# Operand sums built in the second feed-forward's first tiles, one ordinary tile ahead of its second down stage, transposes in pieces, and DRAM sums issued at other steps

## The chip, the cores and the metric

The kernel runs on one core of one Trainium2 chip. The metric is the time of one launch on the device in microseconds (us), as the median of several runs. The core's engines work through queues of their own: PE (TensorE: matrix products into PSUM, and transposes), DVE (VectorE), ACT (ScalarE), POOL (GpSimd) and SP (SyncE, which only starts DMAs). An instruction waits at the head of its queue until its inputs are there and its output buffer is free, and everything behind it on that engine waits with it.

## The reference

One decoder layer on 512 tokens of width 1024, all in float32. The change lies in the last line but one, and in what runs under the line with the mixers:

```python
h = h + FFN_HALF * _swiglu(_rmsnorm(h, norm_ffn1[i]), ffn1_gate[i], ffn1_up[i], ffn1_down[i])
# two attention mixers (native sparse and sliding window), gated and merged:
h = h + merged @ w_out[i]
h = h + FFN_HALF * _swiglu(_rmsnorm(h, norm_ffn2[i]), ffn2_gate[i], ffn2_up[i], ffn2_down[i])
return _rmsnorm(h, norm_final)

def _swiglu(x, w_gate, w_up, w_down):
    return (jax.nn.silu(x @ w_gate) * (x @ w_up)) @ w_down
```

The inner width D_FF is 2816, which is 22 tiles of 128 columns.

## The kernel before, in words

**Products in three passes.** A float32 operand is held as a high part, rounded to the matrix unit's format, and a low part, the rest. A product is three matmuls: high by high, low by high, high by low (`mm3`, L711; `mm` at L386). Splitting an operand costs ACT a copy (the high part) and DVE a subtraction (the low part). A block of weights (128 x 1024 values, 512 KB) is read from DRAM by SP into `raw` and split into `whi` (ACT, L150) and `wlo` (DVE, L154). `W.next()` hands PE the next block and, as it is called, puts the split of the block two places ahead into the queues of ACT and DVE. There are four places for split blocks and four raw buffers.

**Activations.** `uh` and `ul` are the high and low part of h times the norm's gain, 8 blocks of 128 x 512, transposed (features on partitions, tokens along the row). The norm's factor per token is applied later. `norm_in` (L654 to L655) makes them block by block, `square` adds up the squares (ACT, then POOL at L666 into `sqacc`), and `norm_col` and `norm_rows` turn the sum into the factor, with a few small matmuls (printed as `tp`), a chain of tiny DVE steps and one POOL power.

**The output projection.** Eight blocks d = 0 to 7, each 24 matmuls; then DVE adds the result to h (L1763), `norm_in` follows, and for d = 4 to 7 `sums_of_tokens(d - 4)` (L1747 to L1758): from h it forms four combinations of token halves and feature blocks, and splits them into `four_hi` and `four_lo`. They are operands of the fast matrix products of the next stage.

**The second feed-forward** goes over three groups of tiles (0 to 7, 8 to 15, 16 to 21). An *ordinary* tile is 24 matmuls by its gate block, 24 by its up block, and `gated` (L1791 on: DVE takes z from the gate's PSUM bank, ACT silu, DVE t from the up's bank, DVE the product, then a split into rows of `G` or into operands). Tiles 8 to 11, 12 to 15 and 16 to 19 are done four at a time by `four` (L1826 to L1932): seven products of half-size matrices in place of eight, in the order 1, 5, 6, 3, 7, 2, 4, each in two blocks of 12 matmuls (L1857), with tokens on the partitions. Some weight operands of these products are sums of weight blocks that were added up in DRAM beforehand, by DMAs that POOL starts. Results then have to be turned back by transposes (`tp<-ident`, L1889): `pair_rows` turns two tiles' worth, ACT copies them out, and `operands_of` (L1905 to L1916: four DVE combinations, two ACT copies, two DVE subtractions) makes seven operands of the down product from them. Work that is to be put between later matmuls waits in the list `turns`; `turn_back()` takes one entry. Values that `later` holds are put out after the next `W.next()`: the gating of the tokens (L1843).

**Down products.** After the first and the second group, `down` multiplies a group of eight tiles in 14 steps of 12 matmuls with seven-product operands, `left_hi` (rows 0 to 13 of `G`'s storage) and `left["lo"]`. Its steps are (product, half): (1,0), (5,0), (2,0), (1,1), (2,1), (5,1), and so on. The third group's six rows are multiplied at the end by `finish` with ordinary products, 128 tokens at a time, followed by the last norm; its weight blocks base to base+5 are split shortly before.

**What sets the order.** The text of the program alone sets it in this stage: each engine runs what it was given, in that order. In the mixers the order is a list of task numbers written out by hand (`ORDER`, walked by `follow`, L312); every 44th task, `follow` also puts out one POOL DMA for the DRAM sums (`in_mixers`), 24 in all. In the second feed-forward the remaining 16 are put out by `next(steps)`.

Of the kernel before, what the change touches and what calls it, by code (L numbers as in the profile page):

```python
# [15 lines left out]
S = 512  # L16
# [17 lines left out]
FOURS = 8, 12, 16  # L34
# [251 lines left out]
class Schedule:  # L286
# [25 lines left out]
    def follow(self, order, aside, every):  # L312
# [49 lines left out]
def layer(ctx, tc, a, out):  # L362
# [122 lines left out]
    def plan_ffn(n, begun=0, rows=()):  # L485
        lo, hi = UNITS.get(n, (0, 0))
        for f0, f1 in THIRDS:
            for f in range(max(f0, begun), f1):
# [507 lines left out]
    with ExitStack() as mixing:  # L996
# [697 lines left out]
        plan.follow(ORDER, in_mixers(), 44)  # L1694
# [17 lines left out]
        with pool("merge", 2, side="right") as mp:  # L1712
# [30 lines left out]
            minus = mp.tile([128, KD], F32, name="minus", bufs=1)  # L1743
            vector.tensor_scalar(minus, gains[:, 2], -1.0, None, op0=OP.mult)

            def sums_of_tokens(k):


                g1, g2, n1, n2 = (x[:, i:i + 1] for x in (gains[:, 2], minus) for i in (k, 4 + k))
                (h11, h21), (h12, h22) = ((h[:, d, :256], h[:, d, 256:]) for d in (k, 4 + k))  # L1750
                b, p, q = (mp.tile([128, 2, 256], F32, name=name) for name in ("z0", "z1", "z0"))
                scalar.activation(b[:, 0], h21, AF.Identity, scale=g1)
                for o, x, g, y in ((p[:, 0], h22, g2, b[:, 0]), (p[:, 1], h11, g1, b[:, 0]), (q[:, 0], h11, n1, p[:, 0]),
                                   (q[:, 1], h12, n2, q[:, 0])):
                    vector.scalar_tensor_tensor(o, x, g, y, op0=OP.mult, op1=OP.subtract)  # L1755
                for i, x in ((0, p), (2, q)):
                    split(four_hi[:, k, i:i + 2], four_lo[:, k, i:i + 2], x)

            m_in = (lambda k: mh[:, k]), (lambda k: ml[:, k])
            for d in range(KD):  # L1760
                ps = acc(False)
                mm3(ps, W.next(), m_in, KD)
                vector.tensor_tensor(h[:, d], ps, h[:, d], op=OP.add)  # L1763
                norm_in(d, 2)
                if d >= 4:
                    sums_of_tokens(d - 4)


    with pool("temp3", 2) as temp, pool("end") as end:
# [20 lines left out]

        def gated(pg, pu, j, pairs):  # L1791
# [6 lines left out]
            if not pairs:  # L1798
                g = temp.tile([128, 8, 256], F32, name="g", bufs=1).rearrange("p m c -> p (m c)")[:, :S]
                vector.tensor_tensor(g, s, t, op=OP.mult)  # L1800
                split(G[:, j], G[:, 8 + j], g)
# [12 lines left out]
        def operands(g, p):  # L1814
# [9 lines left out]
            vector.tensor_tensor(lo[:, 4:7], g[:, 4:7], f32(hi[:, 4:7]), op=OP.subtract)  # L1824

        def four(j, pairs):  # L1826
# [18 lines left out]
            for m in FOUR_ORDER:  # L1845
# [3 lines left out]
                for kk in range(2):  # L1849
# [9 lines left out]
                    if m == 1 and kk == 1:  # L1859
                        turn_back()  # L1860
                if m == 3:
                    next(steps, None)
                if m in made:
# [54 lines left out]
            def second():  # L1918
                pair_rows(w, False)
                for q in range(2):  # L1920
                    operands_of(q)

            def whole(n):
                ps = turned([(x, n) for x in (*u, *w)])
                split(G[:, j + n], G[:, 8 + j + n], flat(ps))

            if pairs:
                pair_rows(u, True)
                turns.append(second)
# [10 lines left out]
        def down():  # L1940
# [8 lines left out]
            for n, (m, g) in enumerate(STEPS):  # L1949
                if n == 2:  # L1950
# [34 lines left out]
        def finish():  # L1985


            for f in range(6):
                if f == 4:
                    nc.sync.dma_start(left["g_b"], dram(a["norm_final"], 0, [[0, 128], [1, D]]))  # L1990
                    W.prep(base + 1)
                    W.load(base + 5)
                if f == 5:
                    for j in (4, 5, 2):
                        W.split(base + j, 0, 8)
                yield
            W.split(base + 3, 0, 8)
            for t in range(4):
# [4 lines left out]
                for half, (c0, c1) in enumerate(zip(groups, groups[1:])):  # L2003
                    cs = slice(c0, c1)
                    ps = acc(False)[:, :c1 - c0]
                    for n, b in enumerate(LAST_ORDER):
                        j = LAST_ROWS[b]
                        wh, wl = (w.rearrange("p k c -> p (k c)")[:, cs] for w in W.place(base + b))
                        mm(ps, G[:, j, ts], wh, n == 0, False)
                        mm(ps, G[:, 8 + j, ts], wh, False, False)  # L2010
                        mm(ps, G[:, j, ts], wl, False, n == 5)
# [105 lines left out]
```

## Time and profile before

| what | us |
| --- | --- |
| median of 3 runs (1136.84 to 1137.95) | 1137.58 |
| the profiled execution | 1135.84 |
| span in that execution, first to last instruction | 1134.1 |
| PE busy | 1100.2 |
| DVE busy | 759.0 |
| ACT busy | 528.1 |
| POOL busy | 213.9 |

The profiled execution took 1.7 us more than its span, and lies 1.7 us under the median. In the profile's rows a time is the start in us from the first instruction, then a duration; `xN` merges N like instructions; a bracket gives the idle time of the engine before the row and what ended it. `acc`, `o`, `s` and `tp` are PSUM banks (two of each); a matmul of 512 columns is shown with its full latency (0.39 us), while the next one starts about 0.23 us after it. In the tables by windows, PEclk is the clock that PE was granted, as a share of full speed.

### The profile page before, as it was taken

The page shows a single profiled execution, that of the slowest core. Times are in us where ns is not written, and L with a number is a line of the kernel's source. Part 1 is how long each engine was busy: PE and PEld are TensorE (multiplying, and loading weights), DVE is VectorE, ACT ScalarE, POOL GpSimd, SP SyncE. Part 2 cuts the span into 40 slices and gives each one's busy share as a digit, 9 for nine tenths or more (in the row PEclk, how much of TensorE's full clock was granted, in tenths as well). Part 3 has the DMA queues.
Part 4 walks back from the last instruction along what each step waited for, and adds up shares of the span by engine and source line. Part 5 has one row for each costly group of instructions (what it writes and reads, how often), then busy time and mean ns, then how long its engine had stood idle before and what let it go on. Part 6 is the DMA issues. An engine that isn't in the chain of part 4 may idle for free.

```text
span 1134.1 us, 15779 instructions
## 1 busy us (share of the span) xinstructions
PE 1100.2 (97%) x5835; PEld 939.4 (83%) x5835; DVE 759.0 (67%) x1353; ACT 528.1 (47%) x970; POOL 213.9 (19%) x245
## 2 busy tenths in 40 slices
PE   9999999999999999899999999979999998989997
PEld 7888899988888998798888888868888786867776
DVE  5656787854556599987777466584657767686653
ACT  5433344532344466567667534354333435444342
POOL 0211120000003146644434522111110000000002
PEclk9999999999999999899999999989999998999999
DMA  7988979798756367589788557429999654455511
GB/s 211 263 209 219 243 184 266 228 284 258 245 180 176 105 206 224 111 177 288 187 255 218 149 158 204 121 66 246 213 299 238 218 185 135 155 176 188 171 56 75
DMA packets 203205, 220.90 MB, mean 195 GB/s; under 512 B 7700, under 2 KB 160088, under 8 KB 202840
## 3 DMA queue, kind: packets, MB, share of 16 engines
q1 hardware_dynamic: 177208, 156.84, 45.1%
q0 software_dynamic: 23456, 58.72, 22.9%
q10 hardware_dynamic: 2464, 4.33, 1.0%
q8 instruction: 46, 0.75, 0.3%
q14 instruction: 31, 0.25, 0.1%
HBM read 199.94 MB, written 78.64 MB: 246 GB/s over the span
## 4 chain that ended last, share of the span: by engine, by line
PE 87%; DVE 8%; ACT 3%; issue 2%; POOL 0%; POOLq 0%; ACTq 0%; DVEq 0%
PE acc L386 28%; PE s L386 20%; PE o L386 20%; PE o L1857 3%; PE o L782 3%; PE s L1857 2%; PE acc L1857 2%; PE tp L1639 2%; PE s L782 2%; PE acc L782 2%; DVE wlo L154 1%; ACT whi L150 1%; DVE e L1549 1%; DVE z L1755 1%; PE tp L386 1%
## 5 line engine op out<-in xcount | busy, mean ns | idle before, releaser
L154 DVE TENSOR_TENSOR wlo<-raw,whi 128x1024 fp32r<-128x1024 f32 (+2 forms) x219 | 251.4, 1170 | 57.1 <-ACT whi L150 56.7
L150 ACT CAST whi<-raw 128x1024 fp32r<-128x1024 f32 (+2 forms) x244 | 221.7, 934 | 112.8 <-PE o L1857 22.2
L386 PE MATMUL acc<-uh,whi 128*128 128x512 f32 x232 | 93.4, 403 | 0.0
L386 PE MATMUL acc<-uh,wlo 128*128 128x512 f32 x232 | 91.2, 393 | 0.0
L386 PE MATMUL acc<-ul,whi 128*128 128x512 f32 x232 | 91.1, 393 | 0.0
L386 PE MATMUL acc<-whi,uh 128*128 128x256 f32 x224 | 66.2, 295 | 1.3 <-ACT whi L150 1.3
L386 PE MATMUL acc<-wlo,uh 128*128 128x256 f32 x224 | 64.0, 285 | 0.6 <-DVE wlo L154 0.6
L386 PE MATMUL acc<-whi,ul 128*128 128x256 f32 x224 | 63.8, 285 | 0.0
L386 PE MATMUL o<-uh,whi 128*128 128x512 f32 x144 | 57.7, 401 | 1.3 <-DVE z L1882 0.7
L386 PE MATMUL o<-ul,whi 128*128 128x512 f32 x144 | 56.6, 393 | 0.0
L386 PE MATMUL o<-uh,wlo 128*128 128x512 f32 x144 | 56.4, 392 | 0.0
L1654 DVE TENSOR_TENSOR pts<-tp,pts 128x512 fp32r<-128x512 f32 (+1 forms) x62 | 41.9, 687 | 21.1 <-ACT pts L1651 20.4
L386 PE MATMUL s<-uh,whi 128*128 128x512 f32 x136 | 53.2, 391 | 0.0
L386 PE MATMUL s<-ul,whi 128*128 128x512 f32 x136 | 53.0, 389 | 0.0
L386 PE MATMUL s<-uh,wlo 128*128 128x512 f32 x136 | 52.9, 389 | 0.0
L386 PEld LDWEIGHTS acc<-uh,wlo 128*128 128x128 f32 x232 | 43.8, 189 | 9.9 <-DVE wlo L154 0.4
L2021 POOL TENSOR_TENSOR o_t<-o_t,g_b 128x512 f32<-128x512 f32 (+1 forms) x5 | 5.9, 1182 | 241.4 <-ACT z L2015 241.4
L1553 ACT ACTIVATE pbuf<-s,m 128x256 f32<-128x256 f32 (+3 forms) x96 | 47.6, 503 | 8.2 <-DVE c L1563 4.2
L386 PEld LDWEIGHTS acc<-ul,whi 128*128 128x128 f32 x232 | 43.9, 189 | 7.9
L386 PE MATMUL acc<-G,whi 128*128 128x512 f32 x164 | 50.5, 389 | 0.0
L386 PEld LDWEIGHTS acc<-uh,whi 128*128 128x128 f32 x232 | 43.9, 189 | 7.8
L386 PE MATMUL s<-G,whi 128*128 128x512 f32 x160 | 49.3, 390 | 0.0
(465 smaller groups left out, 2953.6 us busy)
## 6 DMA issues: line engine op xcount, KB each, us to landing
raw<-in_ffn_gate_dram SPq DMA_DIRECT2D x42, 512.0 KB, 5.2
raw<-in_ffn_down_dram SPq DMA_DIRECT2D x34, 512.0 KB, 4.9
raw<-in_ffn_up_dram SPq DMA_DIRECT2D x32, 512.0 KB, 6.8
t<-in_ffn_down_dram POOLq DMA_DIRECT2D x12, 1024.0 KB, 9.4
w<-in_ffn_up_dram POOLq DMA_DIRECT2D x12, 1024.0 KB, 9.7
raw<-w SPq DMA_DIRECT2D x24, 512.0 KB, 4.1
raw<-in_w_in_dram SPq DMA_DIRECT2D x20, 512.0 KB, 4.9
raw<-s SPq DMA_DIRECT2D x16, 512.0 KB, 6.4
```

Source lines behind the costliest of these rows:

```text
L150: self.nc.scalar.copy(self.place(i)[0][:, k0:k1], self.raw[i][:, k0:k1])
L154: engine.tensor_tensor(lo, self.raw[i][:, k0:k1], f32(hi), op=OP.subtract)
L386: tensor.matmul(out, lhsT, rhs, start=start, stop=stop)
L782: tensor.matmul(o, a_[:, n], x(k), start=new and n == step == 0, stop=n == 7 and step == 2, skip_group_check=True)
L1549: vector.tensor_tensor(u.e[:, h0], u.m[:, h0], sink[:, 0, u.h0 + hs[0]:u.h0 + hs[-1] + 1], op=OP.add)
L1553: scalar.activation(u.p[:, hd], b.view[:, j], AF.Exp, bias=u.m[:, hd:hd + 1], scale=-1.0, accum_out=u.sum[:, hd:hd + 1])
L1639: tensor.transpose(ps[:w, hd], u.p[:, hd, kb * w:kb * w + w], ident)
L1654: vector.tensor_tensor(p.lo, flat(b.ps)[:w], f32(p.hi), op=OP.subtract)
L1755: vector.scalar_tensor_tensor(o, x, g, y, op0=OP.mult, op1=OP.subtract)
L1857: tensor.matmul(ps, x, y[:, k], start=new and kk == k == step == 0, stop=kk == k == 1 and step == 2, skip_group_check=True)
L2021: gpsimd.tensor_tensor(y, y, left["g_b"][:, cs], op=OP.mult)
```

## The change

Six edits:

1. `sums_of_tokens` leaves the output projection. It is now called once in each ordinary tile f = 0 to 7, at its end, and works from `uh` + `ul`: an even tile does two additions of 128 x 512 and two differences of 128 x 256 and splits them, the odd tile that follows two combinations of 128 x 256 and a split.
2. The groups of tiles become 0 to 7, 8 to 16 and 17 to 21: `four` now takes 8 to 11, 12 to 15 and 17 to 20, and tile 16 is an ordinary tile that runs between `four` of 12 to 15 and the second `down`. Its row is kept in `G[:, 14]` and `G[:, 15]`, which `down` doesn't use. The third group has one ordinary tile, 21, in place of two.
3. In `four` and `down` the transposes and operands go in three entries in place of one: the turning of the second pair, then `operands_of(0)`, then `operands_of(1)`. In `four`, `turn_back` is called after product 1 and after each block of product 5. Around tile 16 the first entry stands after its gate product, the second inside its up product, the third at the start of `down`. After `four` of 17 to 20, two of the four transposes stand after the gate product of tile 21 and two inside its up product.
4. The last stage's weight blocks are prepared in two steps, both in tile 21; the last norm's gain row is loaded in `four`.
5. After `four`, the next PSUM bank is `acc`, where it was `o`.
6. The DRAM sums under the mixers go out at every 64th task up to task 512, then at every 38th.

```diff
-FOURS = 8, 12, 16
+FOURS = 8, 12, 17
+TILES = (0, 8), (8, 17), (17, 22)
...
-            if n % every == every - 1:
+            if n % 64 == 63 if n < 512 else n % 38 == 37:
                 next(aside, None)
...
                 norm_in(d, 2)
-                if d >= 4:
-                    sums_of_tokens(d - 4)
...
+        def sums_of_tokens(f):
+            k, second = f // 2, f % 2
+            tt, stt = vector.tensor_tensor, vector.scalar_tensor_tensor
+            if not second:
+                x, y = tokens["a"] = [temp.tile([128, S], F32, name="y") for _ in range(2)]
+                for o, d in ((x, k), (y, 4 + k)):
+                    tt(o, f32(uh[:, d]), f32(ul[:, d]), op=OP.add)
+                p = tokens["p"] = temp.tile([128, 2, 256], F32, name="t")
+                tt(p[:, 0], y[:, 256:], x[:, 256:], op=OP.subtract)
+                tt(p[:, 1], x[:, :256], x[:, 256:], op=OP.subtract)
+            else:
+                (x, y), s1 = tokens["a"], tokens["p"][:, 0]
+                p = temp.tile([128, 2, 256], F32, name="s")
+                stt(p[:, 0], s1, -1.0, x[:, :256], op0=OP.mult, op1=OP.subtract)
+                stt(p[:, 1], y[:, :256], -1.0, p[:, 0], op0=OP.mult, op1=OP.subtract)
+            split(four_hi[:, k, 2 * second:2 * second + 2], four_lo[:, k, 2 * second:2 * second + 2], p)
...
-                    if m == 1 and kk == 1:
+                    if m == 1 and kk == 1 or m == 5:
                         turn_back()
...
-                turns.append(second)
+                turns.append(lambda: pair_rows(w, False))
+                for q in range(2):
+                    turns.append(lambda q=q: operands_of(q))
...
             for n, (m, g) in enumerate(STEPS):
-                if n == 2:
+                if n == 0:
                     turn_back()
...
-        for third, (f0, f1) in enumerate(THIRDS):
+        for third, (f0, f1) in enumerate(TILES):
             if third == 2:
                 make_room_again()
             for f in range(f0, f1):
                 if any(x <= f < x + 4 for x in FOURS):
                     if f in FOURS:
-                        four(f - f0, third < 2)
+                        four(f - THIRDS[third][0], third < 2)
                         next(steps, None)
-                    if third == 2:
-                        next(last)
-                    if third < 2 and f + 1 == f1:
-                        settle(later)
-                        W.prep(W.pos + 2)
+                        turn[0] = 2
                     continue
+                if third == 2:
+                    settle(later)
+                    next(last)
                 pg = acc(False)
                 wp = W.next()
                 settle(later)
                 mm3(pg, wp, u_in, KD, col if f == 0 else None)
-                for _ in range(2):
-                    turn_back()
+                back(third)
                 pu = acc(False)
-                mm3(pu, W.next(), u_in, KD, rows if f == 0 else None)
-                for _ in range(2):
-                    turn_back()
+                mm3(pu, W.next(), u_in, KD, rows if f == 0 else (lambda: back(third)) if third else None)
...
-                gated(pg, pu, f - f0, third < 2)
+                if third:
+                    gated(pg, pu, f - THIRDS[2][0], False)
+                else:
+                    gated(pg, pu, f, True)
+                    sums_of_tokens(f)
```

Where instructions move shows in the engines' queues. On DVE, in the output projection, before, block d = 4 and the start of d = 5 (`flo` is the low part of the sums, `cols_c` the gains):

```order
L1763 TENSOR_TENSOR h<-s,h 128x512
L655 SCALAR_TENSOR_TENSOR ul<-h,cols_c,uh 128x512
L1755 SCALAR_TENSOR_TENSOR z_7200<-h,cols_c,z_7199 128x256 x2
L1755 SCALAR_TENSOR_TENSOR z_7201<-h,minus,z_7200 128x256
L1755 SCALAR_TENSOR_TENSOR z_7201<-h,minus,z_7201 128x256
L390 TENSOR_TENSOR flo<-z_7200,fhi 128x512
L390 TENSOR_TENSOR flo<-z_7201,fhi 128x512
L154 TENSOR_TENSOR wlo<-raw,whi 128x1024
L1763 TENSOR_TENSOR h<-acc,h 128x512
```

Now, the same two blocks and the one after:

```order
L1748 TENSOR_TENSOR h<-s,h 128x512
L656 SCALAR_TENSOR_TENSOR ul<-h,cols_c,uh 128x512
L155 TENSOR_TENSOR wlo<-raw,whi 128x1024
L1748 TENSOR_TENSOR h<-acc,h 128x512
L656 SCALAR_TENSOR_TENSOR ul<-h,cols_c,uh 128x512
L155 TENSOR_TENSOR wlo<-raw,whi 128x1024
L1748 TENSOR_TENSOR h<-o,h 128x512
```

Six DVE instructions between one block's `ul` and the split of the next weights are gone from each of the last four blocks.

On DVE between `four` of 12 to 15 and the second `down`, before (the gating of `t`, two splits of weights, then both `operands_of`, the second starting at the last row shown):

```order
L1843 SCALAR_TENSOR_TENSOR t<-t,minus,z 128x512 x2
L154 TENSOR_TENSOR wlo<-raw,whi 128x1024 x2
L1909 TENSOR_TENSOR g<-t 128x256
L1910 TENSOR_TENSOR g<-s,t 128x256
L1911 TENSOR_TENSOR g<-g,s 128x256
L1912 SCALAR_TENSOR_TENSOR g<-s,g 128x256
L1915 TENSOR_TENSOR left<-t,G 128x256
L1916 TENSOR_TENSOR left<-g,G 128x1024
L1909 TENSOR_TENSOR g<-t 128x256
```

Now, from the last row of the first `operands_of` on (`z`, `t`, `g` and `G` at L1779 to L391 are tile 16's gating):

```order
L1925 TENSOR_TENSOR left<-g,G 128x1024
L155 TENSOR_TENSOR wlo<-raw,whi 128x1024
L1779 TENSOR_TENSOR z<-acc,r_b 128x512
L1783 TENSOR_TENSOR t<-o,r_b 128x512
L1786 TENSOR_TENSOR g<-s,t 128x512
L391 TENSOR_TENSOR G<-g,G 128x512
L1918 TENSOR_TENSOR g<-t 128x256
```

The first `operands_of` now stands ahead of the reading of tile 16's two PSUM banks, and the second behind it.

On DVE before the last stage, before (`apart` and the `wlo` behind it are the last stage's weights, `G<-tp,G` the turned rows of the four tiles, `z` to `G<-g,G` the gating of tile 20 and then 21):

```order
L390 TENSOR_TENSOR G<-tp,G 128x512 x2
L154 TENSOR_TENSOR apart<-raw,apart 128x1024 x2
L1793 TENSOR_TENSOR z<-o,r_b 128x512
L1797 TENSOR_TENSOR t<-s,r_b 128x512
L1800 TENSOR_TENSOR g<-s,t 128x512
L390 TENSOR_TENSOR G<-g,G 128x512
L154 TENSOR_TENSOR wlo<-raw,whi 128x1024 x3
L1793 TENSOR_TENSOR z<-acc,r_b 128x512
```

Now:

```order
L155 TENSOR_TENSOR apart<-raw,apart 128x1024 x2
L391 TENSOR_TENSOR G<-tp,G 128x512 x4
L155 TENSOR_TENSOR wlo<-raw,whi 128x1024 x3
L1779 TENSOR_TENSOR z<-acc,r_b 128x512
L1783 TENSOR_TENSOR t<-o,r_b 128x512
```

With one ordinary tile left there, the three splits follow right behind the turned rows, the last of which come out of tile 21's own up product.

More of the change, by code (lines that the diff above doesn't have):

```diff
@@ L486, in plan_ffn @@
         lo, hi = UNITS.get(n, (0, 0))
-        for f0, f1 in THIRDS:
-            for f in range(max(f0, begun), f1):
+        for (f0, f1), tiles in zip(THIRDS, TILES if n == 2 else THIRDS):
+            for f in range(max(tiles[0], begun), tiles[1]):
                 if lo <= f < hi:
@@ L1693, in layer @@
         plan.clock["sp"] = plan.clock["store"] = 0.0
-        plan.follow(ORDER, in_mixers(), 44)
+        plan.follow(ORDER, in_mixers())
         W.pos = pos[0]
@@ L1741, in layer @@
                 split(mh[:, d], ml[:, d], y)
[L1743 to L1757, printed above, removed]
             m_in = (lambda k: mh[:, k]), (lambda k: ml[:, k])
@@ L1800, in gated @@
                 vector.tensor_tensor(g, s, t, op=OP.mult)
-                split(G[:, j], G[:, 8 + j], g)
+                split(*rows_of(j), g)
                 return
@@ L1862, in four @@
                     next(steps, None)
+                if m == 3 and not pairs:
+                    nc.sync.dma_start(left["g_b"], dram(a["norm_final"], 0, [[0, 128], [1, D]]))
                 if m in made:
@@ L1916, in operands_of @@
                 vector.tensor_tensor(lo[:, 3:7], g[:, 3:7], f32(hi[:, 3:7]), op=OP.subtract)
[L1918 to L1921, printed above, removed]
             def whole(n):
                 ps = turned([(x, n) for x in (*u, *w)])
-                split(G[:, j + n], G[:, 8 + j + n], flat(ps))
+                split(*rows_of(j + n), flat(ps))
             if pairs:
                 pair_rows(u, True)
-                turns.append(second)
+                turns.append(lambda: pair_rows(w, False))
+                for q in range(2):
+                    turns.append(lambda q=q: operands_of(q))
             else:
@@ L1985, in finish @@
         def finish():
[L1988 to L1996, printed above, removed]
+            W.prep(base + 1)
+            W.load(base + 5)
+            yield
+            for j in (4, 5, 2):
+                W.split(base + j, 0, 8)
+            yield
             W.split(base + 3, 0, 8)
@@ L2008, in finish @@
                         wh, wl = (w.rearrange("p k c -> p (k c)")[:, cs] for w in W.place(base + b))
-                        mm(ps, G[:, j, ts], wh, n == 0, False)
-                        mm(ps, G[:, 8 + j, ts], wh, False, False)
-                        mm(ps, G[:, j, ts], wl, False, n == 5)
+                        gh, gl = (x[:, ts] for x in rows_of(j))
+                        mm(ps, gh, wh, n == 0, False)
+                        mm(ps, gl, wh, False, False)
+                        mm(ps, gh, wl, False, n == 5)
                     y = o_t[:, t, cs]
@@ L2050, in rows, with back @@
             vector.tensor_scalar(minus, norm["col"], -1.0, None, op0=OP.mult)
-        for third, (f0, f1) in enumerate(THIRDS):
+        def back(n):
+            for _ in range(n):
+                turn_back()
+        for third, (f0, f1) in enumerate(TILES):
             if third == 2:
```

5 lines of the change are left out of this document (4 added, 1 removed).

## The prediction

> **What bounds the kernel now.** I read the page first, then PE's waits, then the timeline of the stages that have waits. The page's first lines:
>
> ```profile
> span 1134.1 us, 15779 instructions
> PE 1100.2 (97%) x5835; PEld 939.4 (83%) x5835; DVE 759.0 (67%) x1353; ACT 528.1 (47%) x970; POOL 213.9 (19%) x245
> ```
>
> PE is the bound, and the change neither adds nor removes matmuls. It can only win or lose PE's idle time, 1134.1 - 1100.2 = 33.9 us with the tail in it, and time in which PE runs at a lower clock. PE's list of waits (total, times, longest) names the places:
>
> ```profile
> PE tp L386 <- POOL sqacc L666: 6.4, 1, 6.4
> PE s L386 <- ACT whi L150: 3.9, 2, 2.8
> ...
> PE tp L1639 <- DVE sqacc L1379: 2.9, 1, 2.9
> ```
>
> The first is the norm at the start of the second feed-forward. The second is splits of weights that came late, most of it (2.8) in the second `down`; a like wait of 3.48, in `four` of 12 to 15, stands under B. The last is in the mixers. A wait also costs something behind itself, as the chain that ended last shows around the first one:
>
> ```profile
> 724.85 5.44 PE o L386 x24
> 764.39 2.77 PE acc L386 x6
> 767.16 5.11 PE o L386 x18
> 776.81 5.47 PE s L386 x24
> ```
>
> 24 matmuls of 512 columns take 5.44 (0.227 each); right after the wait, 6 take 2.77 (0.46 each). The table by windows gives the granted clock there, 0.50 (third figure from the end):
>
> ```profile
> 760.00:765.00 5.00, 2.48 (x10) 2.38 (x11) 4.13 (x7) 2.99 (x6) 1.27 (x1) 0.50 0.36 105
> ```
>
> **A: the sums leave the output projection.** The timeline of DVE and POOL there, blocks d = 3, 4 and 7:
>
> ```profile
> 730.32 0.69 DVE L1763 TENSOR_TENSOR h<-o,h 128x512 f32<-128x512 f32 x1 [0.95 <-PE o L386]
> 732.43 1.30 POOL L666 TENSOR_TENSOR sqacc<-sqacc,turn_a 128x512 f32<-128x512 f32 x1 [4.14 <-ACT turn_a L665]
> 738.17 1.68 DVE L1755 SCALAR_TENSOR_TENSOR z<-h,cols_c,z 128x256 f32<-128x256 f32 x2 [0.17 <-ACT z L1752]
> 759.10 0.68 DVE L1763 TENSOR_TENSOR h<-s,h 128x512 f32<-128x512 f32 x1
> 761.21 1.27 POOL L666 TENSOR_TENSOR sqacc<-sqacc,turn_a 128x512 f32<-128x512 f32 x1 [6.47 <-ACT turn_a L665]
> ```
>
> PE ends d = 3 at 724.85 + 5.44 = 730.3, so d = 7 four blocks later, at 752.1. But from d = 4 on the sums (third row) sit in DVE's round, and the last h comes only at 759.10, the last addition of squares at 762.5. Without them DVE follows PE as in d = 3, where POOL was done at 732.43 + 1.30 = 733.7, 3.4 after PE: for d = 7 that is 755.5. PE has 18 matmuls of tile 0 to do first (4.1, to 756.2), so the norm's matmuls wait for nothing and the clock stays up. From there: the norm's sums, 1.9 at half clock (762.5 to 764.39), so 1.0; 24 matmuls at 0.227, 5.4; and what stood between the 18 (to 772.27) and tile 1 at 776.81, 4.5. Tile 1 starts at 767.1, not 776.81. **A gains 9.7.**
>
> The sums must be paid in tiles 0 to 7. The table by windows, and the timeline of tile 7's end:
>
> ```profile
> 768.00:855.00 87.00, 86.52 (x399) 71.61 (x398) 46.18 (x65) 31.11 (x39) 12.37 (x15) 0.99 1.00 258
> 857.86 0.42 DVE L1817 TENSOR_TENSOR g<-g 128x256 f32<-128x256 f32 x1
> 862.19 0.96 DVE L1824 TENSOR_TENSOR left<-g,G 128x768 fp32r<-128x768 f32 x1 [0.90 <-ACT G L1823]
> 863.14 2.36 DVE L154 TENSOR_TENSOR wlo<-raw,whi 128x1024 fp32r<-128x1024 f32 x2
> 866.48 2.80 PE s L386 x12
> ```
>
> On DVE a pair of tiles adds two additions of 128 x 512 (0.69, as h), two differences and two combinations of 128 x 256 (0.42), two subtractions of 0.69, and two waits of about 0.7 for ACT's copy: 5.8, and 23 in all. DVE has 46 in 87; 69 fits. Tight is only the way out of tile 7: its operands end at 863.1, the next split at 864.3, and PE uses it from 866.5 on. The odd tile's sums put 2.2 in between: 866.5, just in time, so I put nothing. If that cover is gone, PE waits up to 2.2 there.
>
> **B: operands in pieces, in `four` of 12 to 15.** Before, both `operands_of` stand ahead of two splits:
>
> ```profile
> 941.87 1.08 ACT L1896 COPY t<-tp 128x512 f32<-128x512 f32 x2 [2.60 <-PE tp L1889]
> 942.49 0.43 DVE L1909 TENSOR_TENSOR g<-t 128x256 f32<-128x256 f32 x1 [0.45 <-ACT t L1896]
> 946.42 0.42 DVE L1909 TENSOR_TENSOR g<-t 128x256 f32<-128x256 f32 x1
> 951.02 0.80 PE L1857 MATMUL o<-whi,fhi 128*128 128x512 f32 x1 [3.48 <-ACT whi L150]
> 956.71 0.47 PE L1857 MATMUL o<-whi,fhi 128*128 128x512 f32 x1
> 959.75 5.60 PE s L1857 x24
> ```
>
> PE waits 3.48 for product 6 from 947.5 on, does its first 12 matmuls in 5.7 (951.02 to 956.71) where the last row has 24 in 5.60, and starts product 3 at 959.75. One `operands_of` takes 3.93 (942.49 to 946.42). Now ACT, after copying out t and product 1 (to 943.9), splits product 6's first block (to 944.9, DVE to 946.1), and PE goes on at 947.5. The first operands run from 946.1 to 950.0, the next split to 951.1 (PE waits 0.3), the second operands to 955.0. Only then does DVE read product 5 from the `s` banks (two of 0.69), and product 3 accumulates into the same banks: PE, ready at 953.5, waits 2.2 to 955.7, does two matmuls, and waits 1.2 for its `wlo` at 957.4. The first block of product 3 ends at 959.7, not at 959.75 + 2.8 = 962.5: 2.8 won. Two waits so close resemble the pair 2.83 and 0.38 under C, behind which 8 matmuls ran slow (0.43 for 0.23, 1.6 in all). **B gains 1.2**, between 0.6 and 2.8.
>
> **C: tile 16 between `four` and `down`.** The start of `down` before, on PE, with DVE's gating of t:
>
> ```profile
> 982.48 0.48 PE L386 MATMUL acc<-whi,G 128*128 128x512 f32 x1
> 986.49 1.41 DVE L1843 SCALAR_TENSOR_TENSOR t<-t,minus,z 128x512 f32<-128x512 f32 x2
> 997.63 0.65 PE L386 MATMUL s<-whi,G 128*128 128x512 f32 x1 [2.83 <-ACT whi L150]
> 999.08 0.79 PE L386 MATMUL s<-wlo,G 128*128 128x512 f32 x1 [0.38 <-DVE wlo L154]
> 1002.48 0.40 PE L386 MATMUL o<-whi,G 128*128 128x512 f32 x1
> ```
>
> Step (5,1) starts at 1002.48; with a tile of 10.9 ahead, 1013.4. Now tile 16's gate product takes PE from 982.5 to 988.0. One more split (1.2) stands ahead of the gating of t, which ends at 989.3, so the transposes wait 1.3 and the up product runs from 990.1 to 995.5. ACT copies t out and splits (992.3), DVE finishes that split at 993.4, the first operands at 997.3, another split at 998.5, and has read the gate's bank (z) only at 999.2. The second half of `down`'s first step needs that bank: PE, there at 996.9, waits 2.3. Tile 16's gating ends at 1001.9, the second operands at 1005.8, the split for step (1,1) at 1007.0, 0.3 late; step (5,1) starts at 1012.1. That is 1.3 won. The new wait of 2.3 lies between one of 1.11 that left the clock alone (under D) and the 2.83 that didn't: I take off half of the 1.6. **C gains 0.5**, between -0.6 and 1.3.
>
> **D: one ordinary tile at the end.** Before:
>
> ```profile
> 1067.50 0.47 PE L386 MATMUL o<-uh,whi 128*128 128x512 f32 x1 [0.69 <-DVE z L1882]
> 1092.22 0.69 DVE L1793 TENSOR_TENSOR z<-acc,r_b 128x512 f32<-128x512 f32 x1
> 1094.86 1.04 ACT L150 CAST whi<-raw 128x1024 fp32r<-128x1024 f32 x1
> 1095.95 0.73 PE L386 MATMUL s<-whi,G 128*128 128x512 f32 x2 [1.11 <-ACT whi L150]
> 1097.55 0.63 PE L386 MATMUL acc<-apart,G 128*128 128x512 f32 x2
> ```
>
> The last weights were split while PE was in tile 21. Now PE needs no `o` bank (0.7 won) and reaches the last stage at 1066.8 + 10.9 + two groups of transposes (0.8 each) = 1079.4. But the second group sits 6 matmuls from the end of tile 21, at 1077.1; ACT copies it out until 1078.8 and splits three blocks until 1081.7, DVE until 1083.4, and z follows. From z to the last `whi` it takes 2.64 (1092.22 to 1094.86): that runs from 1086.0 to 1087.1, its `wlo` to 1088.3. PE waits 0.3, 0.5, 3.45 and 0.75, and its first group ends at 1088.6; before it ended at 1097.55, less tile 20 (10.9) 1086.7. That loses 1.9; and slow matmuls should follow a wait of 3.45 as they did the 3.48: 1.6 more. **D loses 3.5**, between 1.9 and 3.9.
>
> **E: DRAM sums at other tasks.** The 2.9 us wait in the mixers stems from this:
>
> ```profile
> 467.85 1.00 POOL L398 DMA_DIRECT2D w<-in_ffn_up_dram  x1
> 468.01 7.09 DVE L1549 TENSOR_TENSOR e<-m,sink 128x2 f32<-128x2 f32 x1
> 468.53 2.88 POOL L154 TENSOR_TENSOR wlo<-raw,whi 128x512 fp32r<-128x512 f32 x2
> 472.27 2.80 POOL L154 TENSOR_TENSOR wlo<-raw,whi 128x512 fp32r<-128x512 f32 x2
> ```
>
> A DVE step on 128 x 2 values is held until POOL's run of subtractions ends, at 475.07. The DMA inside that run goes elsewhere, which shortens it by 0.7 (467.85 to 468.53). **E gains 0.7**, between -2 (another step caught in the same way, for two POOL instructions) and 6 (rival 1). The Trainium skill's page "SBUF — State Buffer" (Who interferes with whom) says that a DVE instruction with two SBUF inputs and a POOL instruction that reads SBUF lock each other out, and infers that writing a DMA's descriptors does not; by it, E is worth that slot and nothing more. The trace agrees that POOL's subtractions outlast the DMA as the holder.
>
> The new bank, the gain row's load and POOL's other DMAs cost nothing: no row above waits for them. Uncovered, a late 512 KB load would cost about two blocks of matmuls, 5.6.
>
> **The sum.** 9.7 + 1.2 + 0.5 - 3.5 + 0.7 = 8.6. The profiled execution took 1135.84 for its span of 1134.1 and would take 1127.2; the median of the runs is 1.7 above it: 1137.58 - 8.6 = **1129.0**.
>
> The Trainium skill's page "TensorE: Matmul & The Clock Gate" (Part 1) has the clock fall after an idle window of about 3.4 us. By it only D's wait would pay; B and C would gain 2.8 and 1.3, and the time would be 1126.6. The 2.83 us wait, with slow matmuls behind it, speaks against so high a bound.
>
> **Rivals.** (1) In the mixers the DVE step slips in ahead of POOL's run, and with it go the 2.9, a wait behind it and slow matmuls, about 6 more than my E: 1123. For it: the moved DMAs shift both engines by some tenths of a microsecond. Against: the run is several instructions long, and the step must come before its first. 0.16. (2) B, C, D and E all come out at their worst: 9.7 + 0.6 - 0.6 - 3.9 - 2 = 3.8, 1133.8. 0.08. (3) Slower: DVE can't keep up in tiles 1 to 7. A pair of tiles gives PE 21.8; DVE is busy 11.5 of it (46 in four pairs) and waits some more, and would reach about 19 with the sums. If a pair took 24.2, PE would lose 2.4 four times, 9.6: slower than before from there on, and 1139.9 or more from 24.6. The 5.3 that operands and their waits take in each odd tile (857.86 to 863.14) speak for it, the 46 in 87 against. 0.03. (4) The change does not do what it is built to: the norm's wait goes but late weights or late rows of the norm take its place, and gains and losses cancel. 0.03. My own case, from 1125 to 1132, has 0.70.
>
> About 0.2% (2.3 us) can be told from no change. The range 1121 to 1132 holds my case and most of (1). Faster 0.94, same 0.03, slower 0.03.
>
> **What would show it.** Right: no wait of `tp` for `sqacc`, tile 1 some 10 us earlier, no waits in tiles 1 to 7, a wait of about 2 ahead of product 3 (on DVE's reading of `s`) and one in `down`'s first step (on z), and one of over 3 in the last stage's first group. I am wrong if tile 1 comes less than 8 us earlier, if PE waits in tiles 1 to 7, or if the last group has no long wait.

## The result and the profile after

The changed kernel takes **1125.68 us** (median of 4 runs, 1124.33 to 1126.59) against 1137.21 for the kernel before; the ratio is 0.9898, 95% interval 0.9881 to 0.9915, so 9.7 to 13.5 us are won. The forecast was 1129.0 with a range of 1121 to 1132. The profiled execution took 1124.9 for a span of 1123.2, 10.9 less than before. First lines of its page:

```profile
span 1123.2 us, 15782 instructions
PE 1097.0 (98%) x5835; PEld 935.7 (83%) x5835; DVE 753.5 (67%) x1360; ACT 527.1 (47%) x966; POOL 213.3 (19%) x245
```

PE's list of waits (total, times, longest) has no wait of `tp` for `sqacc` any more, neither the 6.4 of the norm nor the 2.9 of the mixers, and four new places:

```profile
PE s L387 <- ACT whi L151: 3.1, 1, 3.1
PE acc L387 <- DVE z L1779: 1.9, 1, 1.9
PE s L1864 <- ACT whi L151: 1.9, 1, 1.9
...
PE s L1864 <- DVE wlo L155: 0.9, 1, 0.9
```

These are the last stage (D), `down`'s first step (C) and product 3 of `four` of 12 to 15 (B, two rows). Around the norm, the chain that ended last shows PE's rows (start, length) from the last block of the output projection to tile 1, and the timeline POOL's last addition of squares:

```profile
744.14 5.60 PE s L387 x24
749.74 4.12 PE acc L387 x18
756.14 4.10 PE o L387 x18
764.79 5.47 PE s L387 x24
...
751.89 1.30 POOL L667 TENSOR_TENSOR sqacc<-sqacc,turn_a 128x512 f32<-128x512 f32 x1 [4.30 <-ACT turn_a L666]
```

PE ends the last block at 749.74, POOL 3.45 later (751.89 + 1.30 = 753.2; the forecast had 3.4), and the norm comes under the 18 matmuls, which stay at 0.229 each. Tile 1 starts at 764.79, 12.0 earlier than before. One thing in these rows was not foreseen: the block takes 5.60, where each block took 5.44 before.

The window of tiles 1 to 7, with DVE's busy time in third place, and the row of PE behind tile 7's way out:

```profile
756.00:843.00 87.00, 86.52 (x401) 71.75 (x400) 60.89 (x94) 34.83 (x46) 12.20 (x14) 1.00 1.00 256
...
854.46 2.98 PE s L387 x12
```

DVE went from 46 to 61 of 87 us, PE's 86.52 did not move, and the tight place costs 0.18 (2.98 for 2.80 in the rows around it).

### The profile page after: what moved, and what is told of

The parts are those of the page before. It is cut to its first block, busy times and chain, and to the rows that moved or that the text cites. A ratio compares the mean times of both kernels' runs of the same rounds, so it can differ in the third digit from the quotient of the medians.

```text
span 1123.2 us, 15782 instructions
## 1 busy us (share of the span) xinstructions
PE 1097.0 (98%) x5835; PEld 935.7 (83%) x5835; DVE 753.5 (67%) x1360; ACT 527.1 (47%) x966; POOL 213.3 (19%) x245
## 4 chain that ended last, share of the span: by engine, by line
PE 89%; DVE 5%; ACT 3%; issue 2%; DMA 0%; POOLq 0%; DVEq 0%; ACTq 0%; SPq 0%
PE acc L387 30%; PE o L387 20%; PE s L387 20%; PE o L1864 3%; PE o L783 3%; PE s L1864 2%; PE acc L1864 2%; PE tp L1640 2%; PE s L783 2%; PE acc L783 2%; DVE wlo L155 1%; ACT whi L151 1%; PE tp L387 1%; DVE turn_a L1338 0%; DMA raw<-in_cmp_k_w_dram 0%
## 5 line engine op out<-in xcount | busy, mean ns | idle before, releaser
L387 PE MATMUL acc<-uh,whi 128*128 128x512 f32 x240 | 96.0, 400 | 0.0
L387 PE MATMUL acc<-uh,wlo 128*128 128x512 f32 x240 | 93.9, 391 | 0.0
L387 PE MATMUL acc<-ul,whi 128*128 128x512 f32 x240 | 93.7, 391 | 0.0
L387 PE MATMUL s<-uh,whi 128*128 128x512 f32 x128 | 49.9, 390 | 0.0
L387 PE MATMUL s<-ul,whi 128*128 128x512 f32 x128 | 49.8, 389 | 0.0
L387 PE MATMUL s<-uh,wlo 128*128 128x512 f32 x128 | 49.8, 389 | 0.0
```

Of the source, the lines that this page charges most:

```text
L387: tensor.matmul(out, lhsT, rhs, start=start, stop=stop)
```

## The experiments

Each kernel was timed beside the kernel before on one chip, and the medians of the kernel before lie between 1136.4 and 1138.5. So kernels are compared with each other by their ratios to it. What a profile says of one place is read from the marks of the chain (the start times of its rows), which are finer than the times.

### E: one DMA in the middle of POOL's run

E gave 3.6 us, not 0.7: the first 24 matmuls in one row of the chain, behind the mixers' last transposes, started at 643.25 and now start at 639.65 (first row). In the changed kernel POOL's run has no DMA in it, and DVE's step on e and m takes 1.15, not 7.09 (0.16 where POOL does not hold it):

```profile
639.65 5.44 PE s L387 x24
...
464.54 6.30 POOL L155 TENSOR_TENSOR wlo<-raw,whi 128x512 fp32r<-128x512 f32 x5 [3.84 <-ACT whi L151]
470.80 1.35 POOL L1178 TENSOR_TENSOR turn_a<-turn_a,turn_b 128x512 f32<-128x512 f32 x1
...
468.46 1.15 DVE L1550 TENSOR_TENSOR e<-m,sink 128x2 f32<-128x2 f32 x1
```

The step does not come ahead of the run, as rival 1 had it: it comes in the middle and gets in when one POOL instruction ends. Either the DMA inside the run or the relative timing could make that difference. Three kernels move one DMA. In `e_min` (the kernel before):

```
-            if n % every == every - 1:
+            if n == 383 if 351 <= n < 395 else n % every == every - 1:
```

> The kernel before, with one DRAM sum moved: the DMA that POOL issued at 467.85, in the middle of its run of subtractions, is issued after that run. Nothing else changes. Theory 1 (the DMA inside the run keeps DVE's step out until the run has ended): this one move is the whole of what the new steps bring in the mixers, 3.6 us, so about 1133.6; DVE's step on e and m no longer lasts 7.09 but falls between single POOL instructions, and the 2.9 us wait of tp for sqacc is gone. Theory 2 (only the relative timing of DVE and POOL, shifted by all the moved DMAs together, decides whether the step is caught): the run starts at the same time as before, the step is caught again, and only the DMA's own slot of 0.7 us is won, about 1136.5, with a hold of some 6.4 us still in the trace.

Measured: 1132.03 (1130.94 to 1134.61, 6 runs), ratio 0.9956, 0.9942 to 0.9971. POOL's five subtractions are one run again, the DVE step takes 1.16, the `sqacc` wait is gone, and the mark at 643.25 came 3.47 earlier:

```profile
464.74 6.31 POOL L154 TENSOR_TENSOR wlo<-raw,whi 128x512 fp32r<-128x512 f32 x5 [3.10 <-ACT whi L150]
...
468.66 1.16 DVE L1549 TENSOR_TENSOR e<-m,sink 128x2 f32<-128x2 f32 x1
```

Theory 1: this one DMA is all of E. `e_plant` does the reverse in the changed kernel:

```
-            if n % 64 == 63 if n < 512 else n % 38 == 37:
+            if n == 351 if 320 <= n < 384 else n % 64 == 63 if n < 512 else n % 38 == 37:
```

> The changed kernel, with one DRAM sum moved the other way: the DMA that comes after POOL's run of subtractions in the mixers (at 478.40) is put after the run's third subtraction. Theory 1 (the DMA inside the run): DVE's step on e and m is held for about 7 us again, tp waits about 3 us for sqacc, and the kernel loses 3.6, about 1129.3. Theory 2 (relative timing): the run starts as in the changed kernel, DVE slips in between POOL's instructions as there, and nothing over 0.7 is lost, 1125.7 to 1126.4.

Measured: 1129.98 (1127.63 to 1131.96, 6 runs), ratio 0.9933, 0.9918 to 0.9948. The hold is back, and with it the wait (PE's list, last row), 3.1 at the mark:

```profile
468.21 0.71 POOL L401 DMA_DIRECT2D t<-in_ffn_down_dram  x1
468.86 2.63 POOL L155 TENSOR_TENSOR wlo<-raw,whi 128x512 fp32r<-128x512 f32 x2
...
468.38 6.81 DVE L1550 TENSOR_TENSOR e<-m,sink 128x2 f32<-128x2 f32 x1
...
PE tp L1640 <- DVE sqacc L1380: 2.9, 1, 2.9
```

In both cases the step came while the DMA was being issued. `e_shift` (340 for 351 in the same line) puts the DMA one subtraction earlier:

> The changed kernel, with the same DRAM sum put into POOL's run of subtractions as in the run where it stood after the third of them, but one place earlier, after the second: the DMA is then over (about 467.7) before DVE's step on e and m comes (468.4). Theory 1a (a DMA anywhere in the run keeps DVE out to the run's end): held for about 6.5 us again, 3 to 4 us lost, about 1129.5. Theory 1b (DVE's step is held only if it comes while POOL is issuing the DMA; POOL's next subtraction then follows without a gap that DVE can use): DVE slips in between the subtractions, at most 0.7 lost, 1125.7 to 1126.4.

Measured: 1131.66 (1129.47 to 1132.64, 5 runs), ratio 0.9941, 0.9928 to 0.9954. Theory 1a:

```profile
467.63 0.73 POOL L401 DMA_DIRECT2D t<-in_ffn_down_dram  x1
468.27 3.88 POOL L155 TENSOR_TENSOR wlo<-raw,whi 128x512 fp32r<-128x512 f32 x3
472.00 1.40 POOL L1178 TENSOR_TENSOR turn_a<-turn_a,turn_b 128x512 f32<-128x512 f32 x1
473.25 2.58 POOL L155 TENSOR_TENSOR wlo<-raw,whi 128x512 fp32r<-128x512 f32 x2
...
469.06 6.80 DVE L1550 TENSOR_TENSOR e<-m,sink 128x2 f32<-128x2 f32 x1
```

The DMA was over at 468.36 and the next subtraction running when the DVE step came at 469.06, and still it waited through the rest of that one and five more, to 475.86. The mark lies at 644.14, 4.5 later than in the changed kernel, more than the 3 to 4 expected. Over the profiled executions whose chain has this row, it starts between 638.48 and 639.90 in the nine where the step is not held, and between 642.77 and 644.14 in the four where it is (before, `a_alone`, `e_plant`, `e_shift`); by the means E is worth 4.2.

The kernel before has a second such place, short enough to have cost nothing that the waits show:

```profile
485.46 1.21 POOL L398 DMA_DIRECT2D t<-in_ffn_down_dram  x1
486.18 1.81 POOL L1256 TENSOR_TENSOR ql<-turn_a,ql 128x512 fp32r<-128x512 f32 x1
487.43 1.25 POOL L1177 TENSOR_TENSOR turn_a<-turn_a,turn_b 128x256 f32<-128x256 f32 x1
...
486.27 2.44 DVE L1562 TENSOR_TENSOR sum<-sum,e 128x2 f32<-128x2 f32 x1
```

So a DMA that POOL issues inside a run without gaps can keep a DVE step on two SBUF tiles out until the run ends; without it DVE waits for one POOL instruction (1.14 to 1.16 in the nine executions without it). All the holds stand among POOL instructions that read two tiles. Where POOL scales one tile by a column, a DMA ahead of it (436.84, in the kernel before) held nothing, and the same DVE step took 0.16 (a like step at 455.10, in the middle of another scaling, took 0.15):

```profile
437.56 1.84 POOL L1574 TENSOR_SCALAR pbuf<-pbuf,c 128x256 f32<-128x256 f32 x2
...
438.52 0.16 DVE L1549 TENSOR_TENSOR e<-m,sink 128x2 f32<-128x2 f32 x1
```

Nor is the hold certain: in `a_alone` the step on sum and e came at 486.59, during the DMA of the second place and ahead of POOL's next instruction at 486.81, and took 0.15. Why a DMA that has been issued holds the step, and when it does not, these runs do not show. The Trainium skill's page "SBUF — State Buffer" (Who interferes with whom) says that the two engines lock each other out for a whole instruction; the 1.15 us agree with that, the 6.8 us over five instructions go beyond it, and the 0.15 and 0.16 among the scalings fall short of it.

### A alone

`a_alone` is the kernel before with `minus` and the sums taken out of the output projection, and the new `sums_of_tokens(f)` called behind `gated` in tiles 0 to 7.

> The kernel before with part A alone: the sums leave the output projection and are made in tiles 0 to 7; the steps of the DRAM sums, four, down and the last stage stay as before. Theory: the norm's wait goes (9.7), tiles 0 to 7 pay nothing, and the output projection's eight blocks take 5.60 instead of 5.44 because the small tile minus is gone and mh and ml begin 32 bytes later (1.3): tile 1 starts 8.4 earlier, about 1128.8, and the waits of four, down and the last stage stand where they stood before. Rival (A's gain needs the earlier part E): tile 1 comes less than 6 earlier. Rival (the sums cost what was allowed for them at the way out of tile 7): 2.2 less, 1131.0.

Measured: 1128.94 (1128.16 to 1129.49, 4 runs), ratio 0.9921, 0.9908 to 0.9934. From the first block of the output projection to tile 1 it takes 59.86 (708.96 to 768.82), before 68.29 (708.52 to 776.81): 8.43, as expected. A needs no other part, and blocks of 5.60 come with it:

```profile
708.96 5.60 PE o L386 x24
...
748.17 5.60 PE s L386 x24
...
768.82 5.47 PE s L386 x24
```

### Why a block takes 5.60: the start address

The table by windows gives the changed kernel's output projection a granted clock of 1.00 (third figure from the end), so the clock is not the reason:

```profile
704.00:750.00 46.00, 46.00 (x199) 36.98 (x198) 26.09 (x29) 17.47 (x24) 7.83 (x6) 1.00 0.36 104
```

What A removed there, beside the sums, is the tile `minus` of 32 bytes per partition, and with it mh and ml start 32 bytes later in the built program: at 139232, 32 past a multiple of 64. `fhi`, `flo`, `left` and `apart` have started at such addresses all along, and there too 24 matmuls take 5.60, in both kernels. `pad_merge` puts 32 bytes back into the pool of mh and ml:

```
+            pad = mp.tile([128, KD], F32, name="pad", bufs=1)
+            vector.memset(pad, 0.0)
```

> The changed kernel, with a tile of 32 bytes per partition in the pool merge alone, in the place of the small tile minus that the change took out there. Only mh and ml move by 32 bytes, to where they were before the change. Theory (the start address decides): the eight blocks of the output projection take 5.44 again instead of 5.60, 1.3 us, about 1124.4, and products 5, 6, 3 and 7 of four and the steps of down stay as they are. Rival (the sums that left the output projection, or what DVE and POOL do now, make its matmuls slower): still 5.60, 1125.7.

`pad_right` puts them ahead of all pools on that side:

```
+        pad = ctx.enter_context(pool("pad", side="right")).tile([128, 8], F32, name="pad")
+        vector.memset(pad, 0.0)
         fours = ctx.enter_context(pool("fours", side="right"))
```

> The changed kernel, with a tile of 32 bytes per partition ahead of the pools fours, h2, merge, left and tail, which shifts all their tiles by 32 bytes; no other instruction changes. In the changed kernel the start addresses of mh, ml, fhi, flo, left and apart are 32 past a multiple of 64 bytes, those of uh, ul, G, whi and wlo multiples of 64. Theory (a matmul with an operand at such an address takes about 233 ns for 512 columns where others take 227): 192 matmuls of the output projection, 288 of the three four, 336 of the two down and 54 of the last stage win about 6.5 ns each, 5.6 in all, so about 1120.1; a block of the output projection takes 5.44 again, and 24 matmuls of products 5, 6, 3 and 7 5.45 for 5.60. Rival (these stages are slow because other engines and DMAs use the memory then): no change, 1125.7, and 5.60 everywhere it was.

and `pad_64` is the same with `[128, 16]`:

> The changed kernel with a tile of 64 bytes, not 32, ahead of the right-hand pools: all their tiles move, but their start addresses stay 32 past a multiple of 64. Theory (the start address modulo 64 decides): a block of the output projection takes 5.60 and 24 matmuls of products 5, 6, 3 and 7 of four 5.60, as without the tile. Rival (any move, or the distance to other tiles, does it): 5.44, as with 32 bytes.

Measured: `pad_merge` 1125.42 (1121.59 to 1130.64, 6 runs), ratio 0.9899, 0.9877 to 0.9922; `pad_right` 1121.53 (1119.04 to 1123.07, 4 runs), ratio 0.9859, 0.9843 to 0.9876; `pad_64` one run, 1127.04. Rows of the chain, the first in the output projection and the second in product 5 or 6 of the first `four`; `pad_merge`:

```profile
703.76 5.44 PE o L387 x24
...
894.21 5.60 PE o L1867 x24
```

`pad_right`, with the row behind B's wait:

```profile
705.11 5.44 PE o L387 x24
...
892.11 5.44 PE o L1866 x24
...
943.12 6.86 PE s L1866 x22
```

`pad_64`, a block of the output projection and one of the first `four`:

```profile
709.48 5.60 PE s L387 x24
...
892.76 5.60 PE o L1866 x24
```

Only the stages whose tiles reach a multiple of 64 become faster, and a move by 64 changes nothing in these two stages: the start address decides. What stays open is `down`. There only every third matmul reads a tile that moved (`left`), yet 24 took 5.60 before and 5.44 in `pad_right` (from 864.42 on): the matmuls between the moved ones became faster too. And in `pad_64` they took 5.55. `pad_right` is 0.39% below the changed kernel, 4.4 us where 5.6 were expected, and the two intervals do not overlap. `pad_merge` can't be told from the changed kernel by time: its runs spread over 9 us, and its profiled execution also had a late load of a weight in the first `down`, which cost 2.8, and slow matmuls behind B's wait.

### B, C and D, and how far a wait slows what follows

`b_undone` makes the transposes and both sets of operands of the first `four` in one lump again:

```
+                rest = [lambda: pair_rows(w, False)] + [lambda q=q: operands_of(q) for q in range(2)]
+                if j == 0:
+                    turns.append(lambda: [x() for x in rest])
+                else:
+                    turns.extend(rest)
...
-                    if m == 1 and kk == 1 or m == 5:
+                    if m == 1 and kk == 1:
```

> The changed kernel with part B undone for four of 12 to 15: the transposes and both sets of operands of four of 8 to 11 are made in one lump behind the first product, as before; the pieces in tile 16 and down stay. Theory (B is worth 1.2, between 0.6 and 2.8): about 1126.9, with one wait of 3.5 for whi in product 6 and about 5.7 for the 12 matmuls behind it, in place of waits of 1.9 and 0.9 in product 3. Rival (the pieces win nothing, since the clock falls behind either wait): 1125.7.

`abe` has A, B and E but FOURS, the tiles and the last stage as before:

> The kernel before with A, B and E, without C and D: four of 16 to 19, tiles 20 and 21 ordinary ones at the end, no tile between four of 12 and down, whose three pending pieces are all made at down's third step as before. Theory (by the marks of the two traces C gained 0.0 and D lost 3.1): about 3 faster than the changed kernel, 1122.7, with the 3.1 us wait of the last stage's first group replaced by one of about 1. Rival (the ordinary tile ahead of down is worth something that the last stage only hides): no faster than the changed kernel, 1125.7 or more.

Measured: `b_undone` 1127.30 (1125.67 to 1127.61, 5 runs), ratio 0.9911, 0.9897 to 0.9924; `abe` 1125.65 (1121.91 to 1127.50, 5 runs), ratio 0.989, 0.9874 to 0.9906. Without B the wait of the kernel before is back, in product 6:

```profile
939.71 0.79 PE L1864 MATMUL o<-whi,fhi 128*128 128x512 f32 x1 [3.49 <-ACT whi L151]
```

Both intervals overlap the changed kernel's. So the times don't settle B, and `abe` missed its 1122.7. Why the times are so blunt is seen behind the waits. PE's row after B's wait in the changed kernel, then the same row in `abe` with its two others that follow a wait:

```profile
945.42 5.39 PE s L1864 x22
```

```profile
944.45 7.85 PE s L1860 x22
...
986.02 4.63 PE s L386 x10
...
1085.92 5.72 PE acc L386 x18
```

The 22 matmuls take 5.1 at 0.233 each. The wait ahead of them is the same, 1.90 for `whi` and 0.6 to 0.9 for `wlo`, yet over the runs with B the row took 5.39, 5.40 and 5.40 (here, `d_early`, `z_early`), 6.86 and 6.93 (`pad_right`, `e_plant`), 7.80 to 8.16 (`e_shift`, `abe`, `pad_64`, `best`, `pad_merge`). Three executions of ten went on at full speed, the others lost up to 2.8. The granted clock goes with it: from 946 to 948 it was 1.00 in the changed kernel and 0.50 in `abe`. Within one kernel the runs differ in the same way: `abe` took 1121.91 at a mean granted clock of 0.995 and 1127.50 at 0.989.

One execution therefore can't price such a part. The stretches between the chain's marks, over all profiled executions with matmuls of 5.60 in `four`, do better: from the last 24 matmuls of the first `four` to those of the second (B), from there to the last `four` (C, less 10.88 where a tile lies between), and from there to the third group of the last stage (D, plus 10.88 where one ordinary tile is left):

| | without the part | with it | part gains |
|---|---|---|---|
| B | 48.4, 48.2, 47.9, 47.2 | 45.7, 47.2, 48.1, 45.7, 45.7, 48.5, 48.1, 48.2 | 0.8 |
| C | 56.9, 56.8, 58.2, 58.1 | 56.9, 56.9, 56.9, 56.9, 55.7, 55.7, 56.6 | 1.0 |
| D | 74.0, 74.0, 74.1, 75.7 | 77.1, 77.4, 77.6, 77.6, 77.4, 78.3, 77.8 | -3.2 |

(`z_early` is left out of C and `d_early` of D. Without B: before, `e_min`, `a_alone`, `b_undone`; without C and D: before, `e_min`, `a_alone`, `abe`.) Only D stands clear of the spread. C's two sets meet at 56.8 to 56.9, and B's overlap so far that 0.8 can't be told from nothing.

A part of the cost lies behind these stretches. From that third group to the end of the span it takes 32.2 to 32.3 in the four executions without C and D, and 32.7 to 33.2 in the eight with them: 0.7 more. The last norm takes the same time in both, the last output DMA is issued 0.3 later, and the rest comes behind it; why is not shown.

### Two repairs, and all together

D's loss should be curable: ACT is idle between the two groups of transposes of tile 21, and the last weights can be split there. `d_early`:

```
-            for j in (4, 5, 2):
+            for j in (4, 2, 5):
                 W.split(base + j, 0, 8)
             yield
-            W.split(base + 3, 0, 8)
+            W.high(base + 3, 0, 8)
+            yield
+            W.low(base + 3, 0, 8, vector)
...
                 back(third)
+                if third == 2:
+                    next(last)
                 pu = acc(False)
```

> The changed kernel, with the splits of the last down weights put elsewhere: three of them (blocks 4, 2 and 5 of the last six) between the two groups of transposes of tile 21, where ACT is idle for 3.9 us, and the fourth's copy ahead of the tile's gating. Theory (D loses because these splits stand behind the second group of transposes): ACT has them done at about 1073.2 and DVE at 1074.7, z follows at once, the wait of 3.1 for whi is gone, and the first group of the last stage ends at about 1081.2 instead of 1085.4 minus what its matmuls ran slow: 4 won, about 1121.6. Rival (the gating of tile 21 itself is what the first group waits for): the wait goes to G of row 5 and the group ends no earlier than 1084.

`z_early` reads the gate's bank at once, in tiles 16 and 21:

```
+                z = gate_of(pg) if third else None
                 pu = acc(False)
...
-                    gated(pg, pu, f - THIRDS[2][0], False)
+                    gated(z, pu, f - THIRDS[2][0], False)
```

> The changed kernel, with one DVE step moved: in tiles 16 and 21 the gate product is read from its bank into z ahead of the up product, not behind it with the second operands in between. Theory (the wait of 1.9 in the first step of down is for this bank alone): the wait is gone, 1.9 won, and up to 1.8 more where the first 18 matmuls behind it ran slow (6.0 for 4.2); the same bank's wait in the last stage does not change. About 1123. Rival (the next split is as late as z): the wait turns into one for whi or wlo of about the same length, 1125.7.

`best` is `pad_right`, `d_early` and `z_early` in one:

> The changed kernel with three edits together: the 32 byte tile ahead of the right-hand pools, the last down weights split between the two groups of transposes of tile 21, and in tiles 16 and 21 the gate product read from its bank (z) ahead of the up product instead of behind it. Theory (the three act in different places and add up): 4 to 5 from the start addresses, 4 to 5 from the last stage, 1.9 to 3 from the wait of 1.9 for z in down's first step and what runs slow behind it: 10 to 13 under the changed kernel's 1125.7, about 1114.5, a ratio to the kernel before of about 0.980. Rival (the waits are only passed on to the next late split or gating): no faster than the better of the two single edits less 1, 1120 or more.

Measured: `d_early` 1121.75 (1119.52 to 1123.31, 5 runs), ratio 0.9857, 0.9842 to 0.9872; `z_early` 1123.51 (1121.47 to 1127.30, 5 runs), ratio 0.9887, 0.9868 to 0.9905; `best` **1115.92** (1114.69 to 1117.92, 4 runs), ratio 0.9816, 0.9802 to 0.983. The changed kernel's last stage shows ACT's three splits, DVE's z and PE's wait; in `d_early` the same splits come 5.2 earlier (1.2 of it from stretch C), and from 1080.75 on 18 matmuls take 4.14, not 5.00:

```profile
1075.08 2.96 ACT L151 CAST whi<-raw 128x1024 fp32r<-128x1024 f32 x3
1079.60 0.68 DVE L1779 TENSOR_TENSOR z<-acc,r_b 128x512 f32<-128x512 f32 x1
1083.33 0.92 PE L387 MATMUL s<-whi,G 128*128 128x512 f32 x2 [3.10 <-ACT whi L151]
1085.38 5.00 PE acc L387 x18
```

In `d_early`:

```profile
1069.91 2.95 ACT L151 CAST whi<-raw 128x1024 fp32r<-128x1024 f32 x3 [0.97 <-DMA raw<-in_ffn_down_dram]
1075.61 0.68 DVE L1779 TENSOR_TENSOR z<-acc,r_b 128x512 f32<-128x512 f32 x1
1080.75 4.14 PE acc L387 x18
```

Stretch D is 72.8 there, 4.8 under the mean of the table. In `z_early` z is read at 973.89 and not at 983.85, but in `down`'s first step PE then waits for a split instead, 0.73 and 0.72 in place of 1.94: in part what the rival had.

```profile
989.61 0.50 PE L387 MATMUL acc<-whi,G 128*128 128x512 f32 x1 [0.73 <-ACT whi L151]
991.05 0.50 PE L387 MATMUL acc<-wlo,G 128*128 128x512 f32 x1 [0.72 <-DVE wlo L155]
```

The stretch C is 1.8 shorter than in the changed kernel (55.1), mostly because nothing runs slow behind the two short waits. The times don't settle it. `best` is 0.83% below the changed kernel, 9.3 us, where 10 to 13 were expected; its row behind B's wait took 7.93. B's wait itself was not removed: by the kernel's text the next product's sums need the buffers that the second operands still hold. More buffers there were not tried.

## Why the prediction was right, and where not

- **A, 9.7.** Right: 12.0 at tile 1, less E's 3.6, is 8.4, and 8 blocks that take 0.16 longer are the other 1.3. What failed is the assumption behind the sum that matmuls which the change doesn't touch keep their duration.
- **Tiles 0 to 7, nothing.** Right: PE's busy time is the same 86.52, 0.18 is lost at tile 7. DVE's 69 in 87 counted waits as well and all four pairs of tiles, where the window holds three and a half; 61 was busy. Rivals 3 and 4 are out.
- **B, 1.2 (0.6 to 2.8).** The waits came where they were said to: 1.90 and 0.93 ahead of product 3, forecast 2.2 and 1.2; there was a third of 0.32. What is lost at a lower clock behind them was put at between nothing and 1.6; it lies between nothing and 2.8, and what decides it is not shown. The mean of the stretches is 0.8, not clear of the spread; the changed kernel's profile alone would say 2.7.
- **C, 0.5 (-0.6 to 1.3).** The wait for z was 1.94, forecast 2.3, and 1.0 is the mean gain; the changed kernel's profile alone would say nothing.
- **D, -3.5 (-3.9 to -1.9).** -3.2, with the wait of 3.10 that was forecast as 3.45. `d_early` shows the cause by taking it away.
- **E, 0.7 (-2 to 6).** This is the term that was mis-sized: 3.6 by the two profiles, 4.2 by the means. The step that failed is "the DMA inside that run goes elsewhere, which shortens it by 0.7": it took the hold to be the run's own, so that only a shorter run could help. The hold was the DMA's. Rival 1 (6 to 6.7) overshot by about as much as the forecast fell short, and its mechanism was wrong too.

With the stretches the sum is 9.7 - 1.3 + 0.8 + 1.0 - 3.2 + 3.6 = 10.6, beside 9.7 to 13.5 by the ratio; the forecast's 8.6 was short by E's 2.9, and the 1.3 of the blocks went the other way. With E at 4.2, and less the 0.2 of tile 7 and the 0.7 behind the last stage, for both of which the forecast had nothing, the sum is 10.3. So the total lies well inside the forecast's range partly because errors of opposite sign met.

Behind the changed kernel's wait of 1.94 for z the granted clock was 0.50 from 986 to 988, and behind B's it was 0.50 in `abe` and 1.00 in the changed kernel. By the idle window of about 3.4 us of the Trainium skill's page "TensorE: Matmul & The Clock Gate" (Part 1) neither B's wait nor C's would slow anything; behind B's 1.9 us seven of ten executions speak against it. That the window runs freely, as the page has it, would make the outcome a matter of chance; the spread of the ten fits that, but no run tests it.

## What to carry to other kernels

Read the start addresses of matmul operands before and after a change: a tile of 32 bytes that comes or goes can shift every operand behind it in its pool, and here a pad of 32 bytes was worth 4.4 us. Issue POOL's DMAs between its runs of instructions on two tiles, not inside one, where a DVE step may then wait for the whole run. And price a wait of PE of about 2 us as a range, over several executions: what it costs behind itself is between nothing and more than its own length.

## What the runs showed of the hardware

- Outside `down`, a matmul of 512 columns took 227 ns where both operands start at a multiple of 64 bytes and 233 where one starts 32 past it, the moving one (mh, ml) as well as the stationary one (fhi, flo): 5.44 against 5.60 for 24, at a granted clock of 1.00. In `down` only every third matmul has such an operand, and all 24 took 5.60 with it and 5.44 without (`pad_right`).
- After a DMA issued by POOL within a run without gaps, a DVE step of 128 x 2 values lasted 6.8 to 7.1 us, over five POOL instructions and more, in four kernels; without the DMA 1.15. Among POOL's scalings by a column it took 0.16, with a DMA ahead of them too.
- Behind the same wait of PE, 1.9 and then up to 0.9 us, 22 matmuls took from 5.39 to 8.16 us in ten executions.
